# A diffusion layer on one core: the first stage's modulation in four column parts, two prompt tiles walked along W together

## The chip, the cores and the metric

One core of a Trainium2 chip runs the whole layer in one launch. The metric is the device time in microseconds (us). A run's time is that of the core; the number compared is the median of several runs of the same program.

## What is computed

One layer of a diffusion backbone, in fp32, for 256 context ("prompt") tokens and 2048 latent ("sample") tokens of width 1024. Cut to what matters here:

```
m  = silu(cvec) @ w_mod + b_mod            # 1024 x 6144, once for c, once for c_ctx
sh1, sc1, g1, sh2, sc2, g2 = split(m, 6)
h  = rms_norm(x, norm1_g) * (1 + sc1) + sh1
p  = h @ w_in                              # 1024 x 2048: q | k | v | fourier channels
q, k = rms_norm(q, q_g), rms_norm(k, k_g)  # per head half of 64; rotary on latent tokens
a  = softmax(q1 k1) - lam * softmax(q2 k2) # per head, 4 heads
x  = x + g1 * (concat[rms_norm(a v), fourier(f)] @ w_out)
x  = x + g2 * (relu(h2 @ w1)**2 @ w2)      # h2: second norm and modulation
```

Context tokens use the vector `c_ctx` and attend to themselves; latent tokens use `c` and attend to 512 cached keys and the 2048 latent ones. New keys and values of the context tokens are outputs too.

## The kernel before

**Arithmetic.** A projection in fp32 is made of three products in the format fp32r: each operand is split in a high part (a rounding copy on ScalarE) and a low part (a subtraction on VectorE), and `mm3` (L85 to L88) issues high x high, high x low and low x high into one PSUM bank. A plain fp32 matmul, where it is used, runs as two passes on TensorE.

**Tiles.** The 18 token tiles of 128 rows (0 and 1 are prompt, 2 to 17 latent) go through the first stage: norm, transposes on TensorE, modulation (scale and shift per column of h, which after the transpose is a scale and bias per partition), split, and four projections of 24 products each (g = 0 q, 1 k, 2 v, 3 fourier). All of W, split in high and low parts, stays in SBUF: 64 tiles of 128 x 512.

**The opening** is a hand-written order (`tc.manual_schedule`), L408 to L517. The first 2048 columns of w_mod (shift1 and scale1) come in eight row blocks of 1 MB, `wm`, L416. For each block TensorE multiplies the block's first three groups of 512 columns (L427: the two vectors are the stationary operand, 128 x 2, the block is streamed), and VectorE accumulates the fourth (L431, L433). Only when all eight blocks have been used are the rows turned into columns (L456 transposes, L461 products with a column of ones), `modc` and `scale1` made (L464, L171, L172), and tile 0 modulated from its transposed copy in PSUM (L472, L474). Then a loop over the eight row blocks k of W splits W[k] (L495 ScalarE, L496 VectorE) and issues for tile 0 the four groups' products with it; W arrives in sixteen halves of 512 KB through six buffers (L446). Tile 1 is transposed at L487 and modulated inside that loop; its projections follow after the loop, one group at a time, with all of W present.

**After the opening** a loop over tiles is put in order by a scheduler: each iteration projects tile i, transposes tile i + 1, and finishes q, k and v of tile i. Every second iteration also loads and computes one of the eight later groups of w_mod's columns (`mod_load`, `mod_group_v`; L163, L165 on VectorE, L167 on TensorE).

**The attention stage** has its events sorted by times that a planner in the code gives them. A group is 256 query rows of one head (two halves j of 128 rows). Per half: score products (L918), row maxima on VectorE (L923, L926), exponentials on ScalarE (L942), and `combine`, which makes P0 - lam * P1 on 128 x 2560 values: usually two pairs of GpSimd instructions (L964, L965: columns 0 to 1023 and 1024 to 2559). Where `vcomb` is not 0 and j is 1, VectorE does the first `vcomb` blocks of 512 columns (L954); with 5 it does all. `vcomb` (L891) is 5 for the very first group and for the last one. The combined rows are transposed on TensorE (L974).

Each engine executes its own queue in order. All loads and stores of the opening are issued by SyncE's queue (SP), also in order: an issue that waits for a buffer holds back those behind it.

Of the kernel before, what the change touches and what calls it, by code (L numbers as in the profile page):

```python
# [10 lines left out]
F32 = mybir.dt.float32  # L11
# [29 lines left out]
def body(tc, a, out):  # L41
    nc = tc.nc
    ctx = ExitStack()
    with ctx:
# [163 lines left out]
        with ExitStack() as c1:  # L208
            p1 = c1.enter_context(tc.tile_pool(name="p1", bufs=2))
            wp = c1.enter_context(tc.tile_pool(name="p1w", bufs=1))  # L210
# [197 lines left out]
            wsrc = a["w_in"][0].rearrange("(k p) n -> p k n", p=P)  # L408
            with tc.manual_schedule():
                with tc.tile_pool(name="p0r", bufs=3) as rows, tc.tile_pool(name="p0m", bufs=KD - 3, side="right") as more:  # L410
                    setup_small(p1, pps)
                    load(0)
                    wm = []
                    for k in range(KD):
                        wm.append((rows if k < 3 else more).tile([P, 2048], F32, tag="row", name=f"wm{k}"))
                        nc.sync.dma_start(wm[k], wmod[:, k, 0:2048])  # L416
                        if k == 2:
                            load(1)
                    norm(p1, X[0], "a0")
                    pr = [pp.tile([P, 512], F32, tag="pj", name=f"pr{gi}", bufs=4) for gi in range(4)]  # L420
                    pt0 = [pp.tile([P, 4, P], F32, tag="pt", name=f"pta0_{b}") for b in range(2)]
                    for k in range(KD):
                        nc.tensor.transpose(pt0[k // 4][:, k % 4, :], X[0][:, k * P:(k + 1) * P], ident)
                    acc = [t2(f"macc3_{s}") for s in range(2)]
                    for k in range(KD):
                        for gi in range(3):
                            nc.tensor.matmul(pr[gi][0:2, :], cols[:, k:k + 9:8], wm[k][:, gi * 512:gi * 512 + 512], start=(k == 0), stop=(k == KD - 1))  # L427
                        for s in range(2):
                            wk, sc = wm[k][:, 1536:2048], cols[:, 8 * s + k:8 * s + k + 1]
                            if k == 0:  # L430
                                nc.vector.tensor_scalar_mul(acc[s], wk, sc)  # L431
                            else:
                                nc.vector.scalar_tensor_tensor(acc[s], wk, sc, acc[s], op0=ALU.mult, op1=ALU.add)  # L433
                        if k == 4:
                            norm(p1, X[1], "a1")
                wr = right.enter_context(tc.tile_pool(name="p1wr", bufs=1, side="right", reuse_waits="tile"))
                W = {(g, x): [(wp if g == 2 else wr).tile([P, 512], F32R, tag=f"w{x}{g}_{k}", name=f"w{x}{g}_{k}") for k in range(KD)]
                     for g in (1, 0, 3, 2) for x in "hl"}
                wh, wl = ([W[g, x] for g in range(4)] for x in "hl")
                with tc.tile_pool(name="p0h", bufs=6, reuse_waits="tile") as halves:  # L440
                    wraw = []

                    def w_half(n):
# [4 lines left out]
                    for n in range(6):  # L448
                        w_half(n)
                    pm = pps.tile([P, 16, 2], F32, tag="pg", name="pm16")  # L450

                    def mod_cols(gi):
                        r = t2(f"mr{gi}")
                        (nc.vector.tensor_copy if gi == 1 else nc.scalar.copy)(r[0:2, :], pr[gi][0:2, :])
                        for j in range(4):
                            nc.tensor.transpose(pm[:, gi * 4 + j, :], r[0:2, j * P:(j + 1) * P], ident[0:2, 0:2])  # L456

                    mod_cols(0)
                    for s in range(2):
                        for j in range(4):  # L460
                            nc.tensor.matmul(pm[:, 12 + j, s:s + 1], acc[s][:, j * P:(j + 1) * P], ones, start=True, stop=True)  # L461
                    mod_cols(2)
                    mod_cols(1)
                    nc.vector.tensor_add(modc[:, 0:16, :], pm, cols[:, 32:48].unsqueeze(2).to_broadcast([P, 16, 2]))  # L464
                    mk_scale(scale1, 8, 80)
                    lq = load_gains(p1)
                    HH.update({i: tuple(p1.tile([P, KD, P], F32R, tag=f"h{x}", name=f"h{x}{i}") for x in "hl") for i in range(2)})

                    def h_mod(dst, pt, k, eng):
                        sc, sh = scale1[:, k, 1:2], modc[:, k, 1:2]  # L470
                        if eng is nc.vector:
                            nc.vector.tensor_scalar(dst, pt[:, k % 4, :], sc, sh, op0=ALU.mult, op1=ALU.add)  # L472
                        else:
                            nc.scalar.activation(dst, pt[:, k % 4, :], AF.Identity, bias=sh, scale=sc)  # L474
# [17 lines left out]
                    for k in range(KD):  # L492
# [12 lines left out]
                        if k == 6:  # L505
                            norm(p1, X[2], "a2")
# [1399 lines left out]
```

## Time and profile before

| what | us |
|---|---|
| median of 3 runs | 2971.24 |
| lowest, highest run | 2971.06, 2977.52 |
| profiled execution | 2976.96 |
| its span, first to last instruction | 2975.1 |
| TensorE busy in the span | 2910.2 (98%) |
| VectorE, ScalarE, GpSimd busy | 2016.3, 1568.3, 1023.9 |

How to read the profile's lines further down: PE is TensorE, PEld its loading of the stationary operand (which overlaps PE), DVE VectorE, ACT ScalarE, POOL GpSimd, SPq the SyncE queue issuing a transfer. `L427` is line 427 of the program. A timeline row gives the start, the duration, the engine and line, the operation, what is written from what, and in brackets how long the engine had been idle and who released it. Equal neighbours are merged (`x48`). A row of the windows view gives, for one stretch of time, each engine's busy time and number of instructions, then the clock granted to TensorE as a share of full speed, the share of time the DMA engines were busy, and GB/s.

### The profile page before, as it was taken

The page shows a single profiled execution, that of the slowest core. Times are in us where ns is not written, and L with a number is a line of the kernel's source. Part 1 is how long each engine was busy: PE and PEld are TensorE (multiplying, and loading weights), DVE is VectorE, ACT ScalarE, POOL GpSimd, SP SyncE. Part 2 cuts the span into 40 slices and gives each one's busy share as a digit, 9 for nine tenths or more (in the row PEclk, how much of TensorE's full clock was granted, in tenths as well). Part 3 has the DMA queues.
Part 4 walks back from the last instruction along what each step waited for, and adds up shares of the span by engine and source line. Part 5 has one row for each costly group of instructions (what it writes and reads, how often), then busy time and mean ns, then how long its engine had stood idle before and what let it go on. Part 6 is the DMA issues. An engine that isn't in the chain of part 4 may idle for free.

```text
span 2975.1 us, 43755 instructions
## 1 busy us (share of the span) xinstructions
PE 2910.2 (98%) x15417; PEld 2518.0 (85%) x15417; DVE 2016.3 (68%) x3379; ACT 1568.3 (53%) x3540; POOL 1023.9 (34%) x839
## 2 busy tenths in 40 slices
PE   8999999989999999999999999999999999999999
PEld 4888887768888888888889999999999888888887
DVE  6666775678888888875458778777776344344554
ACT  4333322678888888864346556556555322232221
POOL 1111112169898989952222333333332000000000
PEclk9999999989999999999999999999999999999999
DMA  7777878512131211215686677676666454445563
GB/s 274 202 195 198 232 197 250 195 52 84 35 110 37 91 53 34 95 50 157 202 252 213 217 240 225 220 237 214 222 199 229 145 170 163 138 145 173 195 216 107
DMA packets 394414, 495.58 MB, mean 167 GB/s; under 512 B 26403, under 2 KB 307056, under 8 KB 391122
## 3 DMA queue, kind: packets, MB, share of 16 engines
q1 hardware_dynamic: 386560, 477.63, 50.5%
q0 software_dynamic: 2992, 7.28, 0.8%
q10 hardware_dynamic: 4642, 7.88, 0.8%
q8 instruction: 122, 2.00, 0.3%
q14 instruction: 98, 0.80, 0.1%
HBM read 315.20 MB, written 179.57 MB: 166 GB/s over the span
## 4 chain that ended last, share of the span: by engine, by line
PE 84%; ACT 8%; DVE 4%; DMA 2%; issue 1%; POOL 0%; SPq 0%; ACTq 0%; DVEq 0%; POOLq 0%
PE Ss L918 8%; PE ps L86 8%; PE ps L87 8%; PE ps L88 8%; PE pj L86 4%; PE pj L88 4%; PE pj L87 4%; PE pts L974 4%; ACT P1s L942 3%; PE po L88 2%; PE po L86 2%; PE po L87 2%; PE pA L1532 2%; PE pA L1534 2%; PE pA L1533 2%; PE pC L1534 2%
## 5 line engine op out<-in xcount | busy, mean ns | idle before, releaser
L923 DVE TENSOR_REDUCE mxs<-Ss 128x1 f32<-128x512 f32 x640 | 419.4, 687 | 86.8 <-PE Ss L918 77.9
L1227 DVE TENSOR_TENSOR sl<-sr,sh 128x768 fp32r<-128x768 f32 x168 | 161.8, 964 | 339.8 <-ACT sh L1226 339.3
L965 POOL TENSOR_TENSOR P0s<-P0s,P1s 128x1024 f32<-128x1024 f32 x124 | 365.7, 2949 | 10.4
L1226 ACT CAST sh<-sr 128x768 fp32r<-128x768 f32 x168 | 140.2, 835 | 424.9 <-PE ps L87 424.9
L942 ACT ACTIVATE P1s<-Ss,mxs 128x512 f32<-128x512 f32 x320 | 217.2, 694 | 69.3 <-DVE mxs L926 69.3
L1574 POOL TENSOR_TENSOR gs<-g,g 128x384 f32<-128x384 f32 x48 | 70.3, 1464 | 483.7 <-ACT g L1544 376.7
L86 PE MATMUL pj<-wh,hh 128*128 128x512 f32 x576 | 229.8, 399 | 0.7 <-ACT fo L374 0.7
L87 PE MATMUL ps<-tlT,sh 128*128 128x512 f32 x585 | 229.3, 392 | 0.0
L86 PE MATMUL ps<-thT,sh 128*128 128x512 f32 x585 | 229.2, 392 | 0.0
L87 PE MATMUL pj<-wl,hh 128*128 128x512 f32 x576 | 227.7, 395 | 0.7 <-DVE wl L496 0.7
L88 PE MATMUL ps<-thT,sl 128*128 128x512 f32 x585 | 227.7, 389 | 0.0
L88 PE MATMUL pj<-wh,hl 128*128 128x512 f32 x576 | 226.7, 394 | 0.0
L942 ACT ACTIVATE P0s<-Ss,mxs 128x512 f32<-128x512 f32 x320 | 215.8, 696 | 7.8 <-DVE mxs L926 7.7
L918 PE MATMUL Ss<-KS1s,Qs 128*128 128x512 f32 x640 | 199.9, 426 | 13.6 <-ACT P0s L942 11.1
L918 PE MATMUL Ss<-KS0s,Qs 128*128 128x512 f32 x640 | 198.7, 423 | 10.5 <-ACT P1s L942 9.4
L974 PEld LDWEIGHTS pts<-ident,P0s 128*128 128x128 f32 x1280 | 158.0, 141 | 51.7 <-ACT ahs L980 5.7
L974 PE MATMUL pts<-ident,P0s 128*128 128x128 f32 x1280 | 193.0, 274 | 6.3 <-DVE alp L1071 4.1
L1543 ACT ACTIVATE g<-uz 128x384 f32<-128x384 f32 x144 | 75.9, 527 | 207.1 <-DVE uz L1566 180.6
L964 POOL TENSOR_SCALAR P1s<-P1s,tots 128x1024 f32<-128x1024 f32 x124 | 166.7, 1344 | 5.6
L985 DVE TENSOR_TENSOR als<-pts,ahs 128x512 fp32r<-128x512 f32 x256 | 163.9, 681 | 5.3 <-ACT ahs L980 5.3
L86 PE MATMUL ps<-ophT,sh 128*128 128x512 f32 x423 | 165.9, 392 | 1.1 <-DVE uz L1566 1.1
L88 PE MATMUL ps<-ophT,sl 128*128 128x512 f32 x423 | 165.7, 392 | 0.0
(613 smaller groups left out, 8216.1 us busy)
## 6 DMA issues: line engine op xcount, KB each, us to landing
sr<-sd SPq DMA_DIRECT2D x84, 768.0 KB, 4.4
a<-in_w SPq DMA_DIRECT2D x184, 256.0 KB, 3.8
sd<-gs SPq DMA_DIRECT2D x192, 192.0 KB, 1.9
sd<-g SPq DMA_DIRECT2D x144, 192.0 KB, 4.1
wm<-in_w_mod SPq DMA_DIRECT2D x32, 512.0 KB, 5.3
Qs<-qd SPq DMA_DIRECT2D x32, 512.0 KB, 3.7
b<-in_w SPq DMA_DIRECT2D x64, 256.0 KB, 5.2
b<-tsum SPq DMA_DIRECT2D x64, 256.0 KB, 4.6
```

The costliest lines, as they stand in the source:

```text
L86: nc.tensor.matmul(ps, lh, rh, start=first, stop=False)
L87: nc.tensor.matmul(ps, lh, rl, start=False, stop=False)
L88: nc.tensor.matmul(ps, ll, rh, start=False, stop=last)
L918: nc.tensor.matmul(S[:, :w], self.Q[:, x, m, j * P:j * P + P], self.hd.KS[m][:, b * 512:b * 512 + w], start=(x == 0), stop=(x == 1))
L923: nc.vector.tensor_reduce(self.mx[j][:, m, b:b + 1], self.S[j, m, b], axis=AX.X, op=ALU.max)
L942: nc.scalar.activation(dst, S, AF.Exp, bias=self.mx[j][:, m, 6:7], accum_out=self.sm[j][:, m, b:b + 1])
L964: nc.gpsimd.tensor_scalar(p, p, tot[:, 3:4], 0.0, op0=ALU.mult, op1=ALU.add)
L965: nc.gpsimd.tensor_add(d, d, p)
L974: nc.tensor.transpose(pt[:, c:c + P], self.p0[j][:, (kb + t) * P:(kb + t + 1) * P], ident)
L985: nc.vector.tensor_sub(t, self.pt[kb], f32(self.A[kb][0]))
L1226: nc.scalar.copy(hi, src)
L1227: nc.vector.tensor_sub(lo, src, f32(hi))
```

## The change

- The modulation's columns are done in four parts s = 0 to 3. Part s is shift and scale of columns 256 s to 256 s + 255, so it serves the row blocks k = 2s and 2s + 1 of W. Each part is loaded as eight tiles of 128 x 512 (256 KB, in rows of 2 x 1 KB) into tiles that W's row blocks 6 and 7 will use later (`wm_load`).
- TensorE makes the modulation directly as columns (`mod_mm`): the loaded tile is the stationary operand, four 128 x 128 pieces per tile, and the two vectors are streamed, two columns wide. The rows, their transposes and VectorE's accumulation go away. `mod_done` adds the bias and makes the scale of that part.
- Both prompt tiles are transposed at the start into four PSUM banks, copied to SBUF, and modulated and split part by part (`h_part`).
- The loop over k now issues for each W[k] seven groups: four of tile 0 and three of tile 1 (`pj_mm`); tile 1's fourth group follows after the loop. Order: parts 0 and 1 of the modulation, k = 0 and 1, part 2, k = 2 and 3, part 3, k = 4 and 5, then k = 6 and 7 with tile 2's transposes.
- W's halves are loaded among the parts; the splits of W[6] and W[7] wait for parts 2 and 3 to have been read.
- The steps that finish tiles 0 and 1 and the projections of tile 2 are written out after that, and the scheduler's loop starts at i = 2; the column group of w_mod that i = 1 computed goes to i = 2.
- `vcomb` of the first attention group is 2 instead of 5: VectorE combines columns 0 to 1023 of its second half, GpSimd the rest.

The diff, cut to its core:

```
+            wr = right.enter_context(tc.tile_pool(name="p1wr", bufs=1, side="right", reuse_waits="tile"))
...
-                        nc.sync.dma_start(wm[k], wmod[:, k, 0:2048])
...
-                    for k in range(KD):
-                        for gi in range(3):
-                            nc.tensor.matmul(pr[gi][0:2, :], cols[:, k:k + 9:8], wm[k][:, gi * 512:gi * 512 + 512], start=(k == 0), stop=(k == KD - 1))
-                        for s in range(2):
-                            wk, sc = wm[k][:, 1536:2048], cols[:, 8 * s + k:8 * s + k + 1]
...
-                                nc.vector.scalar_tensor_tensor(acc[s], wk, sc, acc[s], op0=ALU.mult, op1=ALU.add)
...
+                def wm_load(s):
+                    if s >= 2:
+                        WM[s] = [w_tile(g, x, 4 + s, f"wm{s}_{g}{x}") for g in (1, 0, 3, 2) for x in "hl"]
                     for k in range(KD):
+                        src = wmod[:, k, 0:2 * D].rearrange("p (t c) -> p t c", t=2)
+                        nc.sync.dma_start(f32(WM[s][k]).rearrange("p (t c) -> p t c", t=2), src[:, :, s * 256:s * 256 + 256])
...
+                def mod_mm(s, ks):
+                    if s not in PM:
+                        PM[s] = pps.tile([P, 4, 2], F32, tag="pg" if s == 1 else "pm", name=f"pm1_{s}")
+                    for k in ks:
+                        for j in range(4):
+                            nc.tensor.matmul(PM[s][:, j, :], f32(WM[s][k])[:, j * P:j * P + P], cols[:, k:k + 9:8], start=(k == 0 and j == 0),
+                                             stop=(k == KD - 1), skip_group_check=True)
+
+                def mod_done(s):
...
+                    nc.vector.tensor_add(m, PM.pop(s).rearrange("p (t k) s -> p t k s", t=2), b)
+                    nc.vector.tensor_scalar_add(scale1[:, c, :], m[:, 1], 1.0)
+                    nc.vector.tensor_mul(scale1[:, c, :], scale1[:, c, :], cols[:, 80 + 2 * s:82 + 2 * s].unsqueeze(2).to_broadcast([P, 2, 2]))
...
+                    wm_load(0)
+                    wm_load(1)
+                    for _ in range(4):
+                        w_half()
+                    norm(p1, X[0], "a0")
+                    norm(p1, X[1], "a1")
+                    pT = [pp.tile([P, 2, 2, P], F32, tag="pj", name=f"pT{s}", bufs=4) for s in range(4)]
...
+                    mod_mm(0, range(0, 4))
+                    x_T(0)
+                    mod_mm(0, range(4, KD))
+                    x_T(1)
+                    mod_mm(1, range(KD))
...
+                    def h_part(s):
+                        for j in range(2):
+                            k = 2 * s + j
+                            nc.scalar.activation(xT[s][:, j], xT[s][:, j], AF.Identity, bias=modc[:, k, 1:2], scale=scale1[:, k, 1:2])
+                        for i in range(2):
+                            hi, lo = (x[:, 2 * s:2 * s + 2, :] for x in HH[i])
+                            nc.scalar.copy(hi, xT[s][:, :, i, :])
+                            nc.vector.tensor_sub(lo, xT[s][:, :, i, :], f32(hi))
...
+                    def pj_mm(i, g, k):
+                        mm3(PJ[i, g], HH[i][0][:, k, :], HH[i][1][:, k, :], wh[g][k], wl[g][k], k == 0, k == KD - 1)
+
+                    def pj_step(ks):
+                        for k in ks:
+                            for i, gs in ((0, range(4)), (1, range(3))):
+                                for g in gs:
+                                    pj_mm(i, g, k)
+
+                    wm_load(2)
+                    w_half()
+                    w_half()
+                    h_part(0)
+                    w_cast(0)
...
+                    mod_done(1)
+                    h_part(1)
+                    w_cast(1)
+                    wm_load(3)
...
+                    for k in range(2):
+                        for g in range(4):
+                            pj_mm(0, g, k)
+                            if g < 3:
+                                pj_mm(1, g, k)
+                    w_cast(2)
...
+                    w_cast(3)
...
+                    mod_mm(2, range(KD))
+                    mod_done(2)
+                    h_part(2)
...
+                    pj_step((2, 3))
+                    w_cast(4)
...
+                    w_cast(5)
+                    mod_mm(3, range(KD))
+                    mod_done(3)
+                    h_part(3)
+                    norm(p1, X[2], "a2")
+                    setup_gains(p1, lq)
+                    pj_step((4, 5))
+                    w_cast(6)
+                    w_cast(7)
...
-            for i in range(1, LAST):
+            for i in range(2, LAST):
...
-                    self.vcomb = 5 if self.last else 5 if hd.h == hd.s == g == 0 else 0
+                    self.vcomb = 5 if self.last else 2 if hd.h == hd.s == g == 0 else 0
```

More of the change, by code (lines that the diff above doesn't have):

```diff
@@ L458, in body @@
[L458 to L466, printed above, removed]
@@ new lines, in body @@
+                    x2_T(0)
+                    for k in (6, 7):
+                        for g in (3, 2, 0, 1):
+                            pj_mm(0, g, k)
+                        if k == 6:
+                            x2_T(1)
+                    X.pop(2)
+                    load(4)
+                    HH[2] = tuple(p1.tile([P, KD, P], F32R, tag=f"h{x}", name=f"h{x}2") for x in "hl")
+                    nc.vector.tensor_copy(HH[2][0], hT)
+                    nc.vector.tensor_sub(HH[2][1], hT, f32(HH[2][0]))
```

178 lines of the change are left out of this document (96 added, 82 removed).

## The prediction

> **What bounds the kernel now.** I read the page first, then the busy time in stretches, then TensorE's rows in order of time through the opening.
>
> ```profile
> span 2975.1 us, 43755 instructions
> PE 2910.2 (98%) x15417; PEld 2518.0 (85%) x15417; DVE 2016.3 (68%) x3379; ACT 1568.3 (53%) x3540; POOL 1023.9 (34%) x839
> ```
> ```profile
> 40.00:480.00 440.00, 438.62 (x2115) 364.23 (x2114) 304.40 (x561) 151.09 (x321) 67.11 (x34) 0.99 0.75 201
> ```
>
> From 40 to 480 us TensorE is busy for 438.62 of 440 us: whatever the opening saves there, by starting the projections earlier, goes through to the end of the stage, and each TensorE instruction added there costs its full time. Before 40 us it is otherwise, as its rows in order of time show:
>
> ```profile
> 10.76 22.77 PE L427 MATMUL pr<-wm,cols 128*2 128x512 f32 x48
> 33.81 1.95 PE L461 MATMUL pm<-ones,macc 128*128 128x1 f32 x16
> 38.51 1.79 PE L487 MATMUL pta<-ident,x 128*128 128x128 f32 x8 [2.17 <-DVE hTa L472]
> 39.95 0.78 PE L86 MATMUL pj<-wh,hh 128*128 128x512 f32 x1
> ...
> 45.96 0.39 PE L86 MATMUL pj<-wh,hh 128*128 128x512 f32 x1
> ...
> 62.44 0.39 PE L86 MATMUL pj<-wh,hh 128*128 128x512 f32 x1
> 62.67 1.03 PE L199 MATMUL pta<-ident,x 128*128 128x128 f32 x8
> 63.46 0.48 PE L87 MATMUL pj<-wl,hh 128*128 128x512 f32 x1
> ...
> 65.84 0.40 PE L88 MATMUL pj<-wh,hl 128*128 128x512 f32 x1
> 66.93 0.50 PE L86 MATMUL pj<-wh,hh 128*128 128x512 f32 x1 [0.69 <-ACT fo L374]
> ```
>
> The first projection product starts at 39.95, because all 2048 columns of the modulation must be there first. From the 13th product (45.96) to the 85th (62.44) are 72 steps: 16.48 / 72 = 0.229 us each. The first twelve took 6.01 us where 2.75 would do: 3.26 lost. The step from 65.84 to 66.93 lost 1.09 - 0.23 = 0.86. So before behaves as if its projections had started at 39.95 + 3.26 + 0.86 = **44.1** and never paused. That is the number to beat.
>
> The twelve slow products are a matter of the granted clock (third column from the right):
>
> ```profile
> 31.91:35.33 3.42, 3.42 (x22) 2.02 (x20) 0.68 (x1) 1.10 (x2) 0.00 (x0) 1.00 1.02 416
> 35.33:38.74 3.41, 1.24 (x14) 1.14 (x15) 2.09 (x8) 1.73 (x5) 0.00 (x0) 1.00 0.80 326
> 38.74:42.15 3.41, 2.72 (x11) 2.12 (x10) 3.34 (x7) 3.41 (x8) 0.00 (x0) 0.50 0.02 5
> 42.15:45.57 3.42, 3.42 (x10) 2.64 (x9) 3.42 (x7) 3.42 (x8) 0.00 (x0) 0.50 0.57 181
> 45.57:48.98 3.41, 3.41 (x17) 2.79 (x16) 3.41 (x7) 2.13 (x5) 0.00 (x0) 1.00 0.85 222
> 1325.57:1328.98 3.41, 2.09 (x17) 1.66 (x15) 0.46 (x2) 1.13 (x3) 0.00 (x0) 1.00 0.98 288
> 1328.98:1332.39 3.41, 1.93 (x6) 0.99 (x7) 3.41 (x5) 3.41 (x7) 0.00 (x0) 1.00 0.73 292
> 1332.39:1335.81 3.42, 3.42 (x11) 2.64 (x10) 3.27 (x7) 0.85 (x5) 0.07 (x1) 0.50 0.67 235
> ```
>
> All changes of the clock in this trace lie on a grid of 3.41 us. A slice with 1.24 of 3.41 us busy is followed by half clock, one fully busy (42.15) by full clock. The limit lies near 60%: after 1.93 (57%) the clock falls, after 2.09 (61%) it does not.
>
> **The change, part by part.**
>
> *Start of the modulation.* TensorE needs `cols` and the first 256 KB tile behind both x tiles.
>
> ```profile
> 7.17 0.15 DVE L107 TENSOR_SCALAR cols<-cols 128x1 f32<-128x1 f32 x1
> ```
> ```profile
> 5.76 1.06 ACT L186 ACTIVATE nsqa<-x 128x1024 bf16<-128x1024 f32 x1 [1.04 <-DMA x<-in_x_prompt]
> ```
> ```profile
> 10.00:20.00 10.00, 10.00 (x21) 2.05 (x21) 4.34 (x7) 1.15 (x2) 0.00 (x0) 1.00 1.02 424
> 110.00:120.00 10.00, 10.00 (x45) 8.23 (x44) 6.14 (x13) 1.81 (x3) 1.85 (x1) 1.00 1.00 250
> ```
>
> x0 is there at 5.76; x1, 0.52 MB at 424 GB/s, at 7.0. The rate for rows of 1 KB isn't in the trace: 424 is for rows of 8 KB, 250 for full engines with rows of 512 B and 2 KB mixed. I take 330, about midway, since 1 KB lies between. A tile then takes 0.8 us: start at 7.8. The Trainium skill's "DMA: Bandwidth & Descriptors", Rules for kernel authors, speaks against this edit, since it asks for at least 1 MiB per DMA for full bandwidth and the change goes from 1 MB to 256 KB; by it the rate would be at the low end, which is rival 3.
>
> *Parts 0 and 1.* 2 x 8 x 4 = 64 matmuls in fp32, each two passes (L461 shows 16 for 8 calls): 128 passes with a fresh 128 x 128 stationary tile. The nearest row is the same operation one column wide, inside the projections:
>
> ```profile
> 107.95 1.84 PE L167 MATMUL pm<-ones,macc 128*128 128x1 f32 x16
> 109.65 0.48 PE L88 MATMUL pj<-wh,hl 128*128 128x512 f32 x1
> ```
>
> From 107.95 to 109.65, 16 passes: 0.106 each (L461: 1.95 / 16 = 0.122 at most). 128 x 0.106 = 13.6. Sixteen transposes at 0.10 (eight from 62.67 to 63.46): 1.6. The first of this runs at half clock until one whole slice has been busy, 3.4 to 6.8 us, of which half is lost: 2.6. The walk along W starts at 7.8 + 13.6 + 1.6 + 2.6 = **25.6**.
>
> Its operands must be there. After the last transpose (25.6 - 6.8 = 18.8) ScalarE does two PSUM copies, two activations and two casts, then W[0]'s four casts; the rows of 30 to 66 us give the prices.
>
> ```profile
> L495 ACT CAST wh<-win 128x512 fp32r<-128x512 f32 x32 | 17.6, 626 | 1.8 <-DMA win<-in_w_in 1.6
> ```
> ```profile
> L496 DVE TENSOR_TENSOR wl<-win,wh 128x512 fp32r<-128x512 f32 x32 | 19.8, 686 | 1.3 <-ACT wh L495 1.3
> ```
>
> That is 0.55 us per cast and 0.62 per subtraction. 2 x 0.6 + 4 x 0.45 (half-size, taken between a half and a whole cast) = 21.8, first cast of W[0] 22.4, its low part 23.0: hidden by 2.6 us. W[0] itself: 4.2 MB of parts at 330 GB/s from 7.0 is 19.7, its two halves 22.2. Hidden too, with little margin.
>
> *The walk.* 168 products (96 of tile 0, 72 of tile 1) as in before, at full clock now. One k takes 21 x 0.229 = 4.8 us of TensorE and 4 x 0.62 = 2.5 of VectorE: the splits stay hidden; with four groups per k, as in before, it was 2.7 against 2.5. k = 1 needs `mod_done(1)`, `h_part(1)` and a cast after 25.6: about 0.6 + 1.8 + 1.2 = 29.2, and TensorE comes at 30.4. Behind `mod_done(1)`'s wait on VectorE stand only these. SP's new waits (part 2's tiles for part 0's last read near 18, part 3's for 25.6) come after 24 and 36 us of traffic ahead of them, so nothing queues behind. W[6] and W[7] are split after part 3 is read, near 59, and used near 69.
>
> *Parts 2 and 3* stand between products, so they cost in full: 128 x 0.106 = 13.6, and 0.1 at each of four seams (109.65 to the next product is 0.32 instead of 0.23): 0.4. Their successors on TensorE, k = 2 and k = 4, use modulation that was finished earlier; nothing waits for `mod_done`.
>
> Sum: after behaves as if started at 25.6 + 13.6 + 0.4 = 39.6 against 44.1: **-4.5**. At 0.122 per pass it is -0.4; with the half clock lasting only 3.4 us, -5.4. I take 0.106, the row inside the projections. What VectorE loses (L431, L433) stood beside transfers: nothing. The loop's later work keeps its amounts; the moved column group has VectorE for it.
>
> *The shared combination.* All five blocks of L954, then its last three in a narrower stretch:
>
> ```profile
> 591.77 4.82 DVE L954 SCALAR_TENSOR_TENSOR P0s<-P1s,tots,P0s 128x512 f32<-128x512 f32 x5
> ```
> ```profile
> 594.53 2.06 DVE L954 SCALAR_TENSOR_TENSOR P0s<-P1s,tots,P0s 128x512 f32<-128x512 f32 x3
> 596.52 3.07 DVE L923 TENSOR_REDUCE mxs<-Ss 128x1 f32<-128x512 f32 x5
> ```
> ```profile
> PE Ss L918 <- ACT P1s L942: 9.4, 8, 5.3
> ```
> ```profile
> 588.27 1.55 POOL L964 TENSOR_SCALAR P1s<-P1s,tots 128x1536 f32<-128x1536 f32 x1
> 589.90 3.48 POOL L965 TENSOR_TENSOR P0s<-P0s,P1s 128x1536 f32<-128x1536 f32 x1
> ```
> ```profile
> 607.61 1.05 PE L974 MATMUL pts<-ident,P0s 128*128 128x128 f32 x4
> ```
>
> VectorE's five row maxima wait for its five combinations; TensorE idles up to 5.3 us for exponentials that wait for those maxima. The last three combinations take 2.06 us and go: **-2.0**. Not more, because the first two run to 594.53 beside GpSimd's 589.90 row. GpSimd gets 1.55 + 3.48 = 5.0 after its row of 589.90 ends (593.4), done near 599; TensorE's first transposes of these rows stand at 607.61, so over 6 us of cover hide it even when all comes 2 us sooner; without that cover it would cost up to 5.0. Bounds: 0 to -4 (three at the pace of the first two, (4.82 - 2.06) / 2 = 1.38 each).
>
> **Sum:** -4.5 - 2.0 = -6.5. Made against the profiled execution (2976.96, span 2975.1 and 1.9 around it); it is 5.7 above the median and within the runs shown. From the median: 2971.24 - 6.5 = **2964.7**.
>
> **Rivals.** *1. Weight loads don't hold the clock: slower.* Parts of the modulation stream two columns per 128 x 128 load. If such stretches count as idle, the opening stays at half clock: 128 passes at 0.212 and 16 transposes at 0.21 are 30.5 instead of 17.8, +12.7; the first products then lose 3.3 as in before; parts 2 and 3 each lose the clock after about 3.4 us (32 passes late by 0.106, 3.4) and another 3.3 on the products behind: +13.4. Together +29.4, so 2994. It decides when such a slice counts for less than about 60%. Against it: the slice at 31.91 has 1.5 us of L427, then mostly L461 of this kind, and kept the clock, though 1.5 of 3.42 is 44%; the slice at 1325.57 kept it with 17 short instructions and the one at 1328.98, with 6 long ones, did not. For it: no slice here is filled by such loads alone. The Trainium skill, "TensorE: Matmul & The Clock Gate", Part 4: PE-mode transpose, says transposes don't count as busy in the same way; by analogy it would back this rival, and no run here shows it. *1b.* The start rises to full clock but parts 2 and 3 lose it: +13.4, so 2978.
>
> *2. The gain is eaten at a hand-over.* After the stage, TensorE waits for a transfer:
>
> ```profile
> PE pabE L86 <- DMA c<-in_c: 3.2, 1, 3.2
> ```
>
> If that transfer's time does not move with the stage, up to 3.2 are lost: 2968. Against it: its buffers come free only as the stage ends. *3. Transfers bind.* At 250 GB/s the two parts end at 23.8 and W[0] at 26.3; the first products start near 27.2, W[2] is split just in time at 42: +1.6, so 2966. If small loads cost more still, some us on top.
>
> **How the numbers follow.** Forecast 0.62; rivals 2 and 3 together 0.15; 1b 0.06; 1 0.17. Range: forecast and rivals 2 and 3 lie from 2959 (half clock short, combination at -4) to 2971, 1b reaches to 2982 with the pass cost at its upper end; rival 1 is left out with little more: 2958.5 to 2982. 0.3% is 8.9 us, about what a measurement of this kernel can tell from no change: faster means below 2962.3, a fifth or so of the forecast (0.14); slower means over 2980, rival 1 and half of 1b (0.20); the rest 0.66.
>
> **What would show it.** Right: modulation matmuls 0.11 us per pass with full clock from about 14 us on, first projection product near 25.6, no gap over 1 us to 80, and P1's exponentials in the first attention groups released about 2 us sooner relative to L954's start. Wrong: granted clock 0.50 inside or behind the modulation's stretches; products waiting for `wl`, for `modc` or for w_mod's tiles; GpSimd's combination still running when TensorE wants these rows.

## The result and the profile after

| | before | after |
|---|---|---|
| median, us | 2971.24 | 3014.77 |
| lowest, highest run | 2971.06, 2977.52 | 3012.6, 3017.84 |
| profiled execution | 2976.96 | 3012.6 |
| its span | 2975.1 | 3010.8 |

The changed kernel is slower: the ratio is 1.014, with a 95% interval of 1.0128 to 1.0152. The forecast was 2964.7 us, with a range up to 2982. Rival 1, with a chance of 0.17 and 2994 us, is what happened in the opening. The two profiled executions differ by 35.6 us, and the opening accounts for 22.9 of these, about two thirds. The medians differ by 43.5; the profiled execution of the kernel before took 5.7 us more than its median, so the traces can't show all of this.

The page of the changed kernel first: the busy times of the engines.

```profile
PE 2942.1 (98%) x15597; PEld 2564.5 (85%) x15597; DVE 2004.1 (67%) x3369; ACT 1567.6 (52%) x3543; POOL 1028.9 (34%) x841
```

TensorE's share is 98% as before, and its busy time rose by 32 us for 180 more instructions. That is the first sign that time was lost inside the instructions, not only between them. Its rows in order of time show where (start, duration, engine and line, operation; L440 is `mod_mm`, L473 the prompt tiles' transposes):

```profile
8.81 1.84 PE L440 MATMUL pm<-cols,wm_1h 128*128 128x2 f32 x8 [1.88 <-DMA wm_1h<-in_w_mod]
...
37.60 1.85 PE L440 MATMUL pm<-cols,wm_2l 128*128 128x2 f32 x8
39.31 0.77 PE L86 MATMUL pj<-wh,hh 128*128 128x512 f32 x1
...
43.70 0.40 PE L87 MATMUL pj<-wl,hh 128*128 128x512 f32 x1
...
51.04 0.95 PE L440 MATMUL pm<-cols,wm_1h 128*128 128x2 f32 x8
...
53.63 1.63 PE L440 MATMUL pm<-cols,wm_0l 128*128 128x2 f32 x8
55.12 1.84 PE L440 MATMUL pm<-cols,wm_3h 128*128 128x2 f32 x8
...
61.95 0.77 PE L86 MATMUL pj<-wh,hh 128*128 128x512 f32 x1
...
74.25 0.95 PE L440 MATMUL pm<-cols,wm_1h 128*128 128x2 f32 x8
...
84.55 0.77 PE L86 MATMUL pj<-wh,hh 128*128 128x512 f32 x1
...
95.87 0.60 PE L569 MATMUL pta<-ident,x 128*128 128x128 f32 x4
```

The opening takes 39.31 - 8.81 = 30.50 us, and every 8 passes in it 1.71 (0.213 each): half clock from the first pass to the last. Part 2 starts at 0.1 per pass, and from 53.63 on it is at half clock too; the products behind it start at 0.43 us apiece. (In TensorE's rows a plain fp32 matmul shows two passes, so 8 passes are 4 calls.) The granted clock of these stretches (third column from the right; the trace has no clock record ahead of its first change, so that 1.00 is printed there):

```profile
50.00:62.00 12.00, 12.00 (x71) 11.79 (x69) 0.00 (x0) 0.00 (x0) 0.00 (x0) 0.66 0.61 231
62.00:74.00 12.00, 12.00 (x42) 9.65 (x43) 6.16 (x13) 5.97 (x12) 0.00 (x0) 0.77 0.26 88
74.00:85.00 11.00, 11.00 (x67) 10.93 (x66) 0.24 (x2) 0.00 (x0) 0.00 (x0) 0.67 0.01 1
85.00:96.00 11.00, 11.00 (x44) 8.80 (x44) 7.01 (x21) 7.29 (x15) 0.56 (x1) 0.86 0.02 7
96.00:480.00 384.00, 376.88 (x1817) 311.41 (x1816) 263.94 (x486) 123.34 (x269) 61.74 (x31) 0.99 0.76 200
```

In the first and third rows TensorE is busy all the time, no other engine does anything to speak of, and the clock is 0.66: nothing is waited for, the work itself goes slowly. Behind the opening there is a second loss. The last row shows TensorE busy for 376.88 of 384 us. The kernel before was busy for all of that stretch:

```profile
96.00:480.00 384.00, 384.00 (x1878) 319.99 (x1876) 262.12 (x483) 118.69 (x255) 59.23 (x29) 1.00 0.76 201
```

The view of TensorE's waits between 90 and 485 us in the changed kernel names the gaps, and the rows in order of time one of them with its consequence:

```profile
PE pm L167 <- DVE macc L165: 3.1, 3, 1.6
PE pta L199 <- DVE x L190: 2.4, 1, 2.4
PE pj L86 <- DVE qn L273: 1.0, 1, 1.0
PE pta L199 <- DVE qT0l L307: 0.6, 1, 0.6
```
```profile
440.55 1.05 PE L167 MATMUL pm<-ones,macc 128*128 128x1 f32 x8 [1.58 <-DVE macc L165]
441.81 1.05 PE L167 MATMUL pm<-ones,macc 128*128 128x1 f32 x8 [0.21 <-DVE macc L165]
442.72 0.53 PE L86 MATMUL pj<-wh,hh 128*128 128x512 f32 x1
...
446.44 0.39 PE L86 MATMUL pj<-wh,hh 128*128 128x512 f32 x1
```

Each wait is lost in full, and after this wait, with L167's sixteen weight loads behind it, the clock halves for a slice: the nine products from 442.72 to 446.44 take 3.72 us where 2.06 would do.

One part of the change did what was forecast, the shared combination (VectorE's rows; L1018 are the row maxima):

```profile
628.99 2.84 DVE L1049 SCALAR_TENSOR_TENSOR P0s<-P1s,tots,P0s 128x512 f32<-128x512 f32 x2
631.75 3.07 DVE L1018 TENSOR_REDUCE mxs<-Ss 128x1 f32<-128x512 f32 x5
634.85 0.16 DVE L1021 TENSOR_REDUCE mxs<-mxs 128x1 f32<-128x5 f32 x1
```

From the first combination to the last maximum it is 634.85 - 628.99 = 5.86 us; with five combinations it was 591.77 to 599.62, 7.85. TensorE's wait there fell from 5.3 to 3.3 us: -2.0, as forecast. GpSimd's part ends at 636.8 and TensorE's first transposes of these rows start at 642.8, so it is hidden.

### The profile page after: what moved, and what is told of

Same layout as the page of the kernel before. It is cut to its first block, busy times and chain, and to the rows that moved or that the text cites. A ratio compares the mean times of both kernels' runs of the same rounds, so it can differ in the third digit from the quotient of the medians.

```text
span 3010.8 us, 44167 instructions
## 1 busy us (share of the span) xinstructions
PE 2942.1 (98%) x15597; PEld 2564.5 (85%) x15597; DVE 2004.1 (67%) x3369; ACT 1567.6 (52%) x3543; POOL 1028.9 (34%) x841
## 4 chain that ended last, share of the span: by engine, by line
PE 82%; ACT 8%; DVE 5%; DMA 3%; issue 1%; SPq 0%; POOL 0%; ACTq 0%; DVEq 0%; POOLq 0%
PE Ss L1013 8%; PE ps L86 8%; PE ps L87 8%; PE ps L88 8%; PE pj L86 4%; PE pj L87 4%; PE pj L88 4%; PE pts L1069 4%; ACT P1s L1037 3%; PE po L88 2%; PE po L86 2%; PE po L87 2%; PE pA L1627 2%; PE pA L1628 2%; PE pA L1629 2%; PE pB L1627 2%
## 5 line engine op out<-in xcount | busy, mean ns | idle before, releaser
L1018 DVE TENSOR_REDUCE mxs<-Ss 128x1 f32<-128x512 f32 x640 | 419.3, 686 | 86.7 <-PE Ss L1013 77.7
L1060 POOL TENSOR_TENSOR P0s<-P0s,P1s 128x1536 f32<-128x1536 f32 (+1 forms) x125 | 369.1, 2953 | 10.4
L1059 POOL TENSOR_SCALAR P1s<-P1s,tots 128x1536 f32<-128x1536 f32 (+1 forms) x125 | 168.6, 1348 | 5.7
```

The source lines that it names most:

```text
L1018: nc.vector.tensor_reduce(self.mx[j][:, m, b:b + 1], self.S[j, m, b], axis=AX.X, op=ALU.max)
L1059: nc.gpsimd.tensor_scalar(p, p, tot[:, 3:4], 0.0, op0=ALU.mult, op1=ALU.add)
L1060: nc.gpsimd.tensor_add(d, d, p)
```

## The experiments

**Theory 1:** a stretch of 128 x 128 weight loads with only two columns streamed behind each doesn't hold TensorE's clock, whatever its busy time says. **Theory 2:** these loads are slow in themselves, or for the transfers' sake. **Theory 3:** the late waits have causes of their own. **Theory 4:** they only follow from the late start. Theories 1 and 2 are rivals, and so are 3 and 4.

### How many columns are streamed

Every weight block keeps its load and streams more columns; only two of them are used.

```
-  PM[s] = pps.tile([P, 4, 2], F32, ...)
+  PM[s] = pps.tile([P, 4, N], F32, ...)
-  nc.tensor.matmul(PM[s][:, j, :], f32(WM[s][k])[:, j * P:j * P + P], cols[:, k:k + 9:8], ...)
+  nc.tensor.matmul(PM[s][:, j, :], f32(WM[s][k])[:, j * P:j * P + P], cols[:, k:k + N], ...)
```

N = 120:

> The changed kernel, but each weight block of the modulation streams 120 columns instead of 2 (118 of them are not used; same loads, same count of passes, same output). Theory 1 (a stretch of weight loads with two columns streamed behind each doesn't hold the clock): the passes fall from 0.213 us to about 0.106 after one slice, the walk along W starts near 27 us instead of 39.3, parts 2 and 3 take about 6.8 to 7 us each instead of 10.9 and 10.4, and the products behind them start at 0.229 us instead of 0.43. The sum from the rows of the changed kernel: 12.3 + 2 x 3.7 + 2.7 + 1.7 + 2 = about -26, so near 2987 us beside 3013 for the changed kernel, if the later stalls stay. Theory 2 (the loads are slow in themselves, for the memory's or the transfers' sake): the passes stay at 0.213 us or get longer, time 3013 or more.

Measured: 2993.03 us (four runs; the kernel before took 2973.72 on that chip, ratio 1.0065, 1.0051 to 1.0079). TensorE's rows:

```profile
13.72 1.06 PE L440 MATMUL pm<-cols,wm_0l 128*128 128x120 f32 x8
...
26.18 1.06 PE L440 MATMUL pm<-cols,wm_2l 128*128 128x120 f32 x8
27.01 0.50 PE L86 MATMUL pj<-wh,hh 128*128 128x512 f32 x1
...
40.31 1.04 PE L440 MATMUL pm<-cols,wm_1h 128*128 128x120 f32 x8
...
47.38 0.48 PE L86 MATMUL pj<-wh,hh 128*128 128x512 f32 x1
47.69 0.39 PE L87 MATMUL pj<-wl,hh 128*128 128x512 f32 x1
```

Sixty times the streaming makes it 21.7 us faster (24 when each kernel is taken against the kernel before on its own chip). From 13.7 on 8 passes take 0.89 (0.112 each), the walk starts at 27.01 instead of 39.31, part 2 takes 7.07 instead of 10.91 and the products behind it run at once at 0.23. Same loads, same transfers, same order on SyncE, ScalarE and GpSimd: theory 2 falls. It is 4 short of the 26 expected. Some 3 of that are a wait of 1.23 us for `modc` (L447), which appears at 29.70 now that the start is right, and a slice at half clock behind it. Theory 4 already loses here: the walk starts 12 us earlier, and TensorE's waits between 90 and 500 us still add up to 7.0 us, as against 7.1.

N = 96, 64, 32 and 16:

> As with 120 columns, but 96 columns: the stream fills about three quarters of a pass. Theory 1 with the slices of the kernel before: parts 2 and 3 keep the clock (about 6.8 us each and no half-clock products behind them, -11.8 us against the changed kernel), but the opening doesn't raise it or raises it late (0.213 us a pass at half clock, walk near 39): about 3001 us; with the rise as well about 2987 us. Theory 2: 3013 us.

> As with 120 columns, but 64 columns behind each weight block: the stream fills about half of a pass. Theory 1 with the slices of the kernel before (the clock was kept from about 60% busy and rose only from about 98%): the opening stays at half clock, 0.213 us a pass, walk near 39; parts 2 and 3 lose the clock as with 2 columns; about 3013 us. If any streaming at all were enough: as with 120 columns, about 2987 us. Theory 2: 3013 us.

> As before with 32 columns, a quarter of a pass. Theory 1: 2993 if the bound lies below a quarter, 3013 if above. With 64 columns enough, and nothing in between measured, I expect 2993.

> The changed kernel with 16 columns behind each weight block (the order of all engines is that of the changed kernel). Theory 1, and 64 columns raised and held the clock where 2 did neither: if the share of a pass in which columns stream decides and the bound lies below an eighth, as with 96 columns, near 2993; if it lies between an eighth and a half, as with 2 columns, near 3013. I expect 3013.

| columns | us | opening, per 8 passes | walk starts | part 2 |
|---|---|---|---|---|
| 2 | 3014.77 | 1.71 to the end | 39.31 | half clock from 53.63 |
| 16 | 3016.3 | 1.71 to the end | 39.0 | half clock from 53.5 |
| 32 | 3011.09 | 1.71 to the end | 39.43 | half clock from 55.6 |
| 64 | 2986.01 | 0.89 from 20.1 | 30.74 | full clock |
| 96 | 2993.22 | 0.89 from 13.6 | 26.83 | full clock |
| 120 | 2993.03 | 0.89 from 13.7 | 27.01 | full clock |

(All but 2 and 120 are single runs.) A transpose streams 128 columns in 0.10 us at full clock (the eight at 62.67 in the kernel before), about as long as a weight load takes. So 32, 64 and 96 columns stream for about a quarter, a half and three quarters of a pass; this is an estimate from these rows.

The table shows two bounds, not one. The bound for *keeping* the clock lies between a quarter and a half: parts 2 and 3 lost it with 32 columns and kept it with 64. The bound for *raising* it is higher, as the opening with 64 columns shows:

```profile
13.60 1.91 PE L440 MATMUL pm<-cols,wm_0h 128*128 128x64 f32 x8
...
17.01 1.92 PE L473 MATMUL pT<-ident,x 128*128 128x128 f32 x8
...
20.11 1.06 PE L440 MATMUL pm<-cols,wm_3l 128*128 128x64 f32 x8
```

Counted in slices of 3.41 us from that run's changes of clock, the slice from 13.05 to 16.47 holds nothing but passes with 64 columns, and the clock stayed at half. It rose at 19.88, behind a slice that is half filled by the eight transposes, about 75% streaming by the same estimate. With 96 columns, three quarters, a slice of such passes was enough (13.35). The changed kernel agrees: its slice from 60.72 to 64.13 is busy throughout, the products in it stream from 61.95 on, about 60% of it, and the next slice was at half clock too. So the bound for raising lies near three quarters: about 60% was not enough, about 75% was. The expectation for 64 columns was right on this (the opening doesn't raise the clock by itself) and wrong on keeping it; the one for 32 was wrong. That 64 is nevertheless faster than 96 has another reason: from the first late tiles on the scheduler put loads and VectorE's steps in another order there, and its trace has none of the waits for `macc`, which has to do with theory 3.

The three slices of the kernel before that the prediction weighed fit the lower bound, once streaming is counted instead of busy time:

```profile
1329.78 0.47 PE L86 MATMUL po<-woh,mh 128*128 128x512 f32 x1 [1.66 <-DVE mh L1361]
1330.29 0.50 PE L87 MATMUL po<-wol,mh 128*128 128x512 f32 x1
1331.43 0.50 PE L88 MATMUL po<-woh,ml 128*128 128x512 f32 x1 [0.64 <-DVE ml L1364]
1331.76 0.40 PE L86 MATMUL po<-woh,mh 128*128 128x512 f32 x1
1332.03 0.50 PE L87 MATMUL po<-wol,mh 128*128 128x512 f32 x1
1332.36 0.59 PE L88 MATMUL po<-woh,ml 128*128 128x512 f32 x1
```

The slice from 1328.98 to 1332.39 has five products that stream for 0.229 each, 1.15 us or 34% (estimated from the step of 0.229), and lost the clock, while its busy time of 57% is mostly latency. The slice at 31.91 with its 44% of L427 kept it, and so did the one at 1325.57, where some ten products of 256 columns (0.115 each) and six transposes (0.10 each) make about 50%. So the bound for keeping the clock is near 40% of streaming (between 34% and 44%), not 60% of busy time, and L461's weight loads in the slice at 31.91 need not have counted for anything.

### The late waits

```
-                norm(p1, X[3], "a3")          # between qk_post(1) and squares(2, 0)
+                    norm(p1, X[3], "a3")      # ahead of the last products of tile 1
```
```
-                mg = 3 + (i + 1) // 2
+                mg = 3 + i // 2
-                mods = (i % 2 or i == 2) and mg < 12
+                mods = i % 2 == 0
-                if i in (4, 6, 8, 10): cache_tile((i - 4) // 2)
+                if i in (5, 7, 9, 11): cache_tile((i - 5) // 2)
```

The first edit alone, the second alone and both, on 96 columns; then both on the changed kernel with its two columns:

> The kernel with 96 columns, and the normalization of the fourth tile's rows (X[3]) moved ahead of the last products of tile 1, before the first tile's later work. Theory 3 (the late stalls have a cause of their own: ScalarE and VectorE reach X[3] late): TensorE's wait of 2.4 us for x at line 199 near 102 goes, with the slices at half clock behind it, 3 to 5 us: about 2989 beside 2993.2. Theory 4 (the late stalls are only a consequence of the late start): no change, 2993.

> The kernel with 96 columns, and the eight later column groups of the modulation on every second tile (2, 4, ... 16, the cache tiles on 5, 7, 9, 11) instead of on 2, 3, 5, ... 15. Theory 3 (VectorE has two groups on two tiles in a row, and the loads of the groups stand behind others): TensorE's waits for macc near 140 and 419 go, with the half-clock slices behind them: 5 to 8 us, about 2986 beside 2993.2. Theory 4: no change.

> 96 columns with both moves. Theory 3: the two gains add, 8 to 15 us against 2993.2: 2978 to 2985, and if all of the late stalls go the stage ends as early as in the kernel before, about 2972 to 2976. Theory 4: 2993.

> The changed kernel with its two columns, and both moves of the late work. Theory 1 with theory 3 (the two causes stand side by side): the half clock of the three stretches stays, about 27 us at the start of the stage, and the late stalls go: about 3000 to 3005 beside 3014.8. Theory 4: 3014.8.

| kernel | us | its base | difference |
|---|---|---|---|
| norm moved | 2988.78 | 2993.22 | -4.4 |
| groups on even tiles | 2983.68 | 2993.22 | -9.5 |
| both (11 runs) | 2980.44 | 2993.22 | -12.8 |
| both, two columns | 2996.18 | 3014.77 | -18.6 |

(All but the third row are single runs, and the eleven of the third spread from 2973.75 to 2983.97, so a few us are not told by these times alone; the traces are clearer.) With the norm moved, TensorE's wait of 2.4 us for `x` is gone and one of 1.6 us for `qT0l` has come in; with the groups on even tiles the waits for `macc` are gone and that for `x` stays. Theory 3 holds: the late waits go with their own edits, at full clock as at half clock, and theory 4 falls. With two columns it is 4 us below the 3000 to 3005 expected. The waits that are left on TensorE between 90 and 500 with both edits and two columns, all but those of the next stage:

```profile
PE pta L199 <- DVE qT0l L307: 1.6, 1, 1.6
```

instead of 7.1 us in four lines. Its stretch from 96 to 480, to be read against the last row of the windows above:

```profile
96.00:480.00 384.00, 382.37 (x1865) 318.16 (x1864) 265.05 (x487) 126.95 (x272) 63.38 (x32) 1.00 0.76 201
```

The profiled executions of the last kernel and of the changed one differ by 16.4 us (2996.18 and 3012.6). Of these, 3.05 are no merit of the edits: the first L569 is at 92.82 instead of 95.87, because parts 2 and 3 with the products behind them each spent one slice less at half clock (10.24 and 6.83 us instead of 13.65 and 10.24), depending on where they begin within a slice. That leaves 13, about as much as the 12.8 at full clock. So the two causes stand side by side: undoing the half clock takes off 21.7 us, undoing the late waits with the slices behind them another 13.

The kernel with 96 columns and both edits takes 1.0019 of the kernel before (1.001 to 1.0028). All of the forecast gain should be in it; its trace shows where most of it is lost. The walk starts at 26.93, the first 42 products take 11.38 us where 9.62 would do (mostly the wait of 1.23 for `modc`), parts 2 and 3 take 7.06 each: 26.93 + 1.76 + 14.12 = 42.8 against 44.1, so -1.3 instead of -4.5. Then come the wait of 1.6 above and one of 0.7 for `macc`, with a slice at half clock, that before doesn't have. A last part comes behind the stage: from the first product of `pabE` to the first of `pabo` (the next stage) it takes 17.95 us where the kernel before takes 14.31, with two waits that the latter doesn't have:

```profile
500.73 0.50 PE L86 MATMUL pabE<-c,E_h 128*128 128x512 f32 x1 [1.50 <-ACT E_h L723]
508.95 0.50 PE L86 MATMUL pabo<-s,O_h 128*128 128x512 f32 x1 [1.32 <-DVE ablE L768]
```

The changed kernel takes 17.13 there. Why ScalarE and VectorE come later with these two tiles was not looked into.

Two more edits went after these waits: tile 1's group in the bank that `modc` frees comes last in k = 0 and 1, and the fourth tile's transposes come behind a further projection.

> 96 columns with both moves of the late work, and two more: at k = 0 and 1 the products of tile 1 with the column group that reuses the bank of part 1's sums come last (TensorE waited 1.23 us there for the modulation to be read out), and the fourth tile's transposes come behind the third column group's products (they waited 1.63 us for a bank). Theory 3 (each of these waits is lost in full, since TensorE is saturated): 2.9 us less than with both moves, 2977 to 2978 beside 2980.4. A rival: what waits is moved, and the time stays.

Measured 2982.92 us (a single run, within the spread of the eleven): no gain. The trace bears the rival out. The wait for `modc` is gone (first products at 27.45 without one), but the wait of 1.6 us became a longer one, and the clock halves for a slice behind it (116.60 to 120.01):

```profile
115.23 1.25 PE L199 MATMUL pta<-ident,x 128*128 128x128 f32 x8 [2.49 <-DVE kT1l L307]
```

The transposes of keys, queries and tiles share two PSUM banks; whichever comes last waits for VectorE to empty one.

### The clock from the start

```
+  for _ in range(24): nc.tensor.transpose(pw, ident, ident)   # ahead of the rows' transpose
+  for _ in range(10): nc.tensor.transpose(pw, ident, ident)   # behind it
```

> The same with 34 transposes of the identity on TensorE before the first loads arrive (24 ahead of the transpose of the small rows, 10 behind it), which write a bank that nobody reads. Theory 1 (the clock follows the work of the slice before): the opening runs at full clock from its first pass, 2.6 to 2.9 us less than without: 2974 to 2975.5 if the run without gives 2977.5; about as long as the kernel before. Rival (the clock rises only after a fixed time from the start): no change.

Measured 2984.13 us (five runs; ratio to the kernel before 1.0037, 1.0023 to 1.005): not faster than 2982.92, the single run without them. But theory 1's clock is there:

```profile
8.28 1.10 PE L445 MATMUL pm<-cols,wm_1h 128*128 128x96 f32 x8 [0.29 <-DMA wm_1h<-in_w_mod]
9.24 1.10 PE L445 MATMUL pm<-cols,wm_1l 128*128 128x96 f32 x8
...
19.02 1.06 PE L445 MATMUL pm<-cols,wm_0h 128*128 128x96 f32 x8
22.32 2.02 PE L445 MATMUL pm<-cols,wm_0l 128*128 128x96 f32 x8 [2.24 <-DMA wm_0l<-in_w_mod]
```

The first passes run at full clock. Then, at 20 us, TensorE has caught up with the transfers: it waits 2.24 us for a tile of part 1, loses the clock, and the walk starts at 29.73, later than without. This is rival 3 (transfers bind), which only shows once the clock is not the bound. The rate in that stretch is the last number of this row:

```profile
8.28:22.00 13.72, 11.80 (x104) 11.63 (x104) 3.89 (x10) 2.85 (x7) 4.12 (x7) 0.99 1.05 266
```

266 GB/s with tiles of 256 KB; from 8.5 to 22 us the other traces with this order of loads show 259 to 297, the DMA engines full in all of them. That is at the low end of what the prediction weighed (250 to 424), not the 330 that it took. The first 2.6 us at half clock are thus covered by transfers and can't be saved by a warm TensorE alone.

### The same two ideas in the kernel before

Two instead of five combinations on VectorE, nothing else:

> The kernel before with one edit: in the first group two instead of five heads' combinations on VectorE, the others on GpSimd. If the 2.0 us between the two traces at this place (7.85 us from the first combination to the first transpose copy, 5.86 in the changed kernel) is a gain of its own: 2969.2 us beside 2971.2, ratio 0.9993. If GpSimd's share is given back later: no difference. GpSimd's part ended 3.5 us ahead of its next work in the changed kernel's trace, so I expect the first.

Measured 2971.72 us against 2973.72 (11 and 15 runs): 0.9995, 0.9986 to 1.0004. The 2.0 us are there in its trace (TensorE's longest wait for P1's exponentials is 3.3 instead of 5.3 us), but neither they nor nothing can be excluded in the time.

Filling the wait ahead of the first products, and that together with the shared combination:

```
   mod_cols(1)
+  for _ in range(20): nc.tensor.transpose(pw, ident, ident)
```

> The kernel before with one edit: 20 transposes of the identity (128 x 128 each, into a bank that nobody reads) on TensorE between the modulation's last small transposes and tile 1's transposes, where it waits 2.2 us. All engines keep their order. Theory 1 (the clock of a slice follows what was streamed in the slice before): the clock stays up over 38.74, tile 1's transposes take 0.8 us instead of 1.5 and the first products 0.229 us; TensorE then still waits for the first low part of W near 41.4, so 2.1 to 2.6 us are gained: 2971 beside 2973.4, ratio 0.9991 to 0.9993. Rival (the clock falls for another reason, or transposes don't count as work): no change.

> The same, and two instead of five combinations on VectorE in the first group. If both gains are real they add: 4.1 to 4.6 us, 2969 beside 2973.4, ratio 0.9985 to 0.9986, faster than both kernels. If the shared combination's 2.0 us are given back later: as without it.

Measured: 2974.8 against 2975.24 (0.9997, 0.9988 to 1.0006), and 2973.14 (0.9992, 0.9983 to 1.0001). Neither is clear of no change. TensorE's rows of the first of them:

```profile
34.78 0.65 PE L456 MATMUL pm<-ident,mr 2*128 2x2 f32 x8
35.36 3.61 PE L463 MATMUL pw<-ident 128*128 128x128 f32 x20
38.76 1.54 PE L487 MATMUL pta<-ident,x 128*128 128x128 f32 x8
40.06 0.47 PE L86 MATMUL pj<-wh,hh 128*128 128x512 f32 x1
...
58.08 0.51 PE L87 MATMUL pj<-wl,hh 128*128 128x512 f32 x1 [0.58 <-DVE wl L496]
61.45 1.09 PE L199 MATMUL pta<-ident,x 128*128 128x128 f32 x8 [0.30 <-DVE x L190]
```

The clock still fell, one slice earlier (L461's weight loads fill most of the slice ahead of 36.37), and the transposes brought it back by 40: the products run at full clock from the first, 2.8 us ahead at the thirteenth. That fits theory 1. But 0.9 of the 2.8 is luck: the row of L456 that ends the modulation stands at 34.78 instead of 35.68, ahead of the added transposes, because the clock happened to rise sooner while w_mod was streamed (12.48 instead of 14.84). And only 1.2 of the 2.8 were left at 66 us, because TensorE now waits for VectorE's splitting of W (0.58) and for a tile's norm (0.30). The 3.3 us at half clock, part of the 44.1 to beat, were partly cover for VectorE. No kernel of this study is clearly faster than the kernel before.

## Why the prediction was wrong

**The step that failed** is "The first of this runs at half clock until one whole slice has been busy, 3.4 to 6.8 us, of which half is lost: 2.6", and with it the price of 0.106 for all 256 passes. A slice of weight loads with two columns behind each did not count as work in any run, so the clock never came: 128 passes and two groups of transposes took 30.50 us at half clock where 17.8 were forecast. Term by term:

| term | forecast | measured | difference |
|---|---|---|---|
| start of the modulation | 7.8 | 8.81 | +1.0 |
| parts 0 and 1 with the transposes | 17.8 | 30.50 | +12.7 |
| first products, 39.31 to 43.70: ten steps less 10 x 0.229 | 0 | 2.1 | +2.1 |
| part 2 with its seams | 7.0 | 10.91 | +3.9 |
| 42 products behind it: 12.30 less 9.62 | 0 | 2.7 | +2.7 |
| part 3 with its seams | 7.0 | 10.30 | +3.3 |
| 42 products behind it: 11.32 less 9.62 | 0 | 1.7 | +1.7 |

That is 39.6 + 27.4 = 67.0 against 44.1: +22.9. Rival 1 had +29.4 on the forecast for this. It had the opening to the tenth (30.5) and the parts within 0.5; the products were too dear (3.3 each, for 2.1, 2.7 and 1.7), in part a matter of where each stretch falls in the slices. That its 2994 is still 21 us below the measured time has the other cause, below.

**The evidence against rival 1 was misread.** "The slice at 31.91 has 1.5 us of L427, then mostly L461 of this kind, and kept the clock" was taken as weight loads that count. It kept the clock by its 44% of streaming. "Less than about 60%" was the bound in busy time; in streaming it is near 40% for keeping the clock. That raising it takes more was to be seen in the prediction's own table: the slice at 38.74 was busy for 2.72 of 3.41 us at half clock, and the next one stayed there. The row of 0.106 per pass (107.95) was no witness either: sixteen such passes among products are over before the slice ends. The Trainium skill's "TensorE: Matmul & The Clock Gate", Part 4: PE-mode transpose, from which the rival was given an analogy, says that transposes don't count as busy in the same way; the runs say otherwise for these fp32 transposes, whose 128 columns stream: 34 of them ahead of the first pass had the clock up (8 passes in 0.96 us at 8.28). The analogy pointed the right way for a wrong reason.

**"The moved column group has VectorE for it" was wrong**, and "no gap over 1 us to 80" was right only because it ended at 80. From 96 on 12.4 us were lost, for which the sum had zero: at the stage's end TensorE stood 35.3 us later than before (520.85 for 485.59, the starts of its wait for `pabE`), and the opening accounts for 22.9 of them. The two edits gave 13 back, the slices at half clock included. The working looked at VectorE's mean load. What counted was the place: two column groups on two tiles in a row (i = 2 and 3), the norm of X[3] behind the first tiles' copies on ScalarE, and perhaps the loads and splits that the scheduler arranged around them, which no run tested apart.

**Right:** the shared combination, -2.0, in every trace that has it, and that GpSimd's part is hidden. In the span it doesn't show, since from the stage's end to the first combination the changed kernel loses 2.0 more (108.14 us instead of 106.18). That is near rival 2, a loss at a hand-over, but not by its mechanism: the longest wait there is 3.7 us instead of 3.2 and is put down to VectorE, not to a transfer.

**Half right: the transfers.** They did not bind in the changed kernel, but only because TensorE was slow. Small tiles came at 259 to 297 GB/s, between rival 3's 250 and the 330 of the sum. (The sum's 22.2 for W[0]'s two halves holds at 424 GB/s; at its 330 it would be 22.9.) The Trainium skill's "DMA: Bandwidth & Descriptors", Rules for kernel authors, which asks for at least 1 MiB per DMA, agrees with that row in direction. Rows of 1 KB instead of 8 KB came with the smaller tiles, so no run here tells which of the two costs the rate.

**Would the forecast have held at full clock?** Only in part. With the clock and the late waits mended, the start of the stage gained 1.3, not 4.5: the passes took 0.112 instead of 0.106 (+0.7 over 128), the first tile came 0.7 later, and the first 42 products lost 1.8, 1.23 of it in a wait for a PSUM bank that was not seen. "Hidden too, with little margin" left no margin at all.

Open: what delays ScalarE and VectorE in the next stage, by 3 to 5 us in the traces with the new opening, how much of the spread of the late waits lies with the scheduler's order rather than with the two edits, and whether the shared combination alone is worth 2 us in the time.

## What to carry to other kernels

Read what a stretch streams, not how busy TensorE looks: here 128 x 128 weight loads with a few columns behind them filled the engine's time at half speed and left the work behind them at half speed as well. A matrix-by-two-vectors product should rather stream the matrix; else it took half as many streamed columns as loaded ones to keep the clock, and three quarters to raise it. Where one engine is saturated, a moved step is paid at the place it is moved to: check which queue it joins and what stands there already, tile by tile, not the mean load. And a stretch that is slow for one reason covers the next bound: at full clock from its first pass this opening waits for its transfers, and the products of the kernel before for VectorE.

## What the runs showed of the hardware

- A pass with a fresh 128 x 128 fp32 weight block takes 0.213 us at half clock and 0.112 at full clock with 2 as with 120 columns: the load follows the granted clock.
- The clock goes by the columns streamed in a slice of 3.41 us, not by TensorE's busy time, and with two bounds. With a quarter of the pass streaming (32 columns) it neither rose nor held; with half (64) it held but didn't rise (13.05 to 16.47 of that run); with three quarters (96) it rose.
- fp32 transposes with an identity count as work for the clock: 34 of them on an otherwise idle TensorE had it at full clock by 8.28 us.
- A wait of 1.6 us among products left the clock up (the kernel with both edits, 102.22); one of 1.58 us with sixteen weight loads behind it (440.55 of the changed kernel) halved it for a slice, another 1.66 us.
